# A hybrid SSM and attention block: the order of instructions on every engine read from a table instead of worked out by a planner in the kernel

## The chip, the cores and the metric

The kernel runs on one core of a Trainium2 chip. Its time is the device time of one execution in microseconds. The kernel before took 1474.67 us (median of three runs, 1472.99 to 1477.0).

## The reference

One layer (DEPTH 1, BATCH 1, 2048 tokens, width 1024, f32) of a block with two mixers side by side, cut to its core:

```python
hn = rmsnorm(h, mix_norm_g)
u, g_ssm, q, k, v, g_attn = split(hn @ w_in)          # six times 512 columns
y_ssm = s5_branch(u, ...) * silu(g_ssm)               # 32 groups of 16 channels, 64 complex states each, then GELU and GLU
y_att = stick_breaking_branch(q, k, v, ...) * silu(g_attn)
h = h + concatenate([y_ssm, y_att]) @ w_out
h = h + sigmoid(rmsnorm(h, ple_norm_g) @ w_ple_gate) * (p @ w_ple_proj)
```

Stick-breaking attention, for each of 8 heads of 64 and each block of 128 queries, causal, with q and k normalised per head:

```python
z = einsum(qb, kb) * scale
log_stay = where(strict, log_sigmoid(-z), 0)
later = cumsum(log_stay, reverse) - log_stay
weights = where(strict, exp(log_sigmoid(z) + later), 0)
out = einsum(weights, vb)
```

## The kernel before, in words

Matrices are multiplied in three passes: every operand is split into a rounded high half and what is left of it (`split`, ACT for the high half in L513, DVE for the low half in L65; weights with their norm's scale in L491 on ACT and L76 on DVE, in `load_w`), and `mm3` (L541 to L543) or `mm3x` (L707 to L709) adds high by high, high by low and low by high in one PSUM bank.

The work goes in stages, which overlap at their edges.

- `phase_u` (0 to about 130 us in the trace) makes u for the SSM in eight tiles of 256 tokens, T=0 to 7, in the banks `ps_u`. For T=0, x is loaded already turned (L561), in pieces, beside the first weights (`wst`, `w_w`), and its norm is applied to the result (`norms`: squares L575 on ACT, sums L577 on POOL, `ps_row`, `rs0`, `dg`). For T=1 to 7 each half tile (128 tokens, L593) is squared (L596 on ACT), normalised (L598 on ACT), turned by 16 transposes on PE (L526, `ps_x`) and split into `xt` (L513 on ACT, L65 on DVE), which is also kept in memory (`hn`, L602). Results leave PSUM in L635 (ACT, `uq`). DVE works beside it on the chain of small tables for the SSM (`ssm_chain`, tiles `ex`, `sc`, `pr`).
- The SSM (130 to 315 us) multiplies with packed matrices of the state space, and `gate_unit` makes its gate (`ps_sg`).
- Attention (315 to 1090 us) goes over four passes of two heads each, skewed against each other. `attn_proj` (L745, `ps_q`) projects one block of 128 tokens; ACT and DVE join its two halves (`part`, `qn`); L756 on POOL takes differences of v after a DMA has put the neighbour row in place (`v`); ACT squares, DVE sums, L507 on POOL raises to the power -1/2 (`rs_qk`), DVE multiplies (`qn<-qn,rs_qk`), PE transposes (`ps_tq`) and q, k and the gate are split. `attn_block` makes the scores (L812, `ps_z`), a sigmoid (ACT L816, `px`), a mask (POOL L819), a running product from the right (DVE L821), transposes (L526, `ps_wt`), copies (L835, `ws`), and multiplies with the differences of v (L843, `ps_o`). Between these lie the units of the GLU (`glu_unit`, `ps_g2` and `ps_v2`, its last product L698 on POOL) and `cross_sums`, which makes sums and differences of weight blocks (L874 to L877 on POOL, tiles `old`) for a seven-product scheme.
- `phase_out` (to 1473 us) multiplies with w_out (`mixed_pair`, `ps_h`) and with the gate's weights (`gated_pair`, `ps_t` for transposes, L1000; `ps_g`, `ps_p`) by the seven products of `cross_products`, with `yr` the split operand.

The program text builds these stages one after the other. The order in which each engine takes its instructions is set afterwards by `arrange`, which chains every engine's instructions by a dependency without a semaphore from each to the next: PE, ACT, DVE, POOL and SP (which issues most of the DMAs) each follow their line. In the kernel before, the line comes from a planner. `plan` reads the data dependencies from the instructions' access patterns and gives each a cost (`duration`). `best_order` runs `list_schedule` six times, forwards over the program with ranks from a backward run: at each step the engine that is free first takes the instruction of best rank that is due, with a bonus of `near=4.0` for PE staying in the same tile shape and a cost of `change=0.09` for leaving it. It keeps the order with the earliest end. Hints in the program text (`first`, `later`, `mark`) move ranks and hold back DMAs, and runs marked `abreast` (the halves of a tiled matmul, transposes) stay together.

Of the kernel before, what the change touches and what calls it, by code (L numbers as in the profile page):

```python
# [18 lines left out]
P = 128  # L19
# [1262 lines left out]
def footprint(ap, offset, shape):  # L1282

    row = 1
    for n in shape[1:]:
        row *= n
    p0, m = offset // row, 1
    f = offset % row + sum((n - 1) * s for s, n in ap[1:] if s < 0)
    for s, n in ap[1:]:
        if s and n > 1:  # L1290
            m = sum(m << (abs(s) * k) for k in range(n)) if n * abs(s) > 64 or m != 1 or s not in (1, -1) else (1 << n) - 1
    return p0, p0 + ap[0][1], m << f


def duration(i, name, outs, ins, psum):

    n = max([a[1] for a in outs + ins] or [1])
    eng = str(i.engine).split(".")[-1]
    if name == "InstDMACopy":
        names = [a.bass_ap.tensor.name for a in i.ins if getattr(a, "bass_ap", None) is not None]  # L1300
        return (0.6 if eng == "Pool" else 0.45), (4.0 if any("ssm_w_glu" in k for k in names) else 0.0)
    if name == "InstMatmult":
        cols, kind = outs[0][1], ins[0][2]
        if i.is_transpose:
            return (0.031 if ins[0][0] <= 64 else 0.109), 0.11
        if "float32r" in kind or "bfloat16" in kind:
            return max(cols / 2400.0 + 0.0136, 0.107) / (2 if ins[0][0] <= 64 else 1), 0.11
        half = min(outs[0][0], ins[0][0]) <= 64
        return (0.5 if outs[0][0] <= 32 else 1 if half else 2) * max(cols / 1160.0, 0.056), 0.12
    if eng == "Activation":  # L1310
        return (0.05 if psum else 0.094) + n * 0.00083, 0.065 if psum else 0.03
    if eng == "Pool":
        if name == "InstTensorTensor" and "pow" in str(i.op).lower():
            return 0.35 + 0.15 * n, 0.08
        base, slope = {"InstMemset": (0.04, 0.0008), "InstTensorCopy": (0.4, 0.001), "InstTensorScalarPtr": (0.25, 0.001), "InstTensorScalarAffineSelect": (0.14, 0.0008)}.get(name, (0.12, 0.00186))
        return base + slope * n, 0.09
    if name == "InstTensorScalarPtr" and i.is_tensor_tensor_scan:
        return 0.05 + n * 0.0022, 0.03
# [304 lines left out]
```

## Time and profile before

| | before |
|---|---|
| median of three runs | 1474.67 us |
| profiled execution | 1474.24 us |
| its span in the trace | 1472.5 us |
| mean granted clock of TensorE | 0.994 |
| busy: PE, DVE, ACT, POOL | 98%, 69%, 55%, 32% |
| instructions | 33586 |
| HBM read, written | 166.94 MB, 64.90 MB |

All rows of the trace come from the one profiled execution; its own time is longer than the span since a start and an end lie around the span. A row of the timeline gives start and length in us, the engine, the line, what is written and read, and in brackets the idle time ahead of it with what ended it. PE is busy when any matmul is under way, and matmuls overlap, so the pace is read from start to start.

### The profile page before, as it was taken

Reading aid. Unit: us, or ns where it says so; the run is one execution under the profiler, and the core shown is the slowest. Engines: PE = TensorE matmul, PEld = TensorE weight load, DVE = VectorE, ACT = ScalarE, POOL = GpSimd, SP = SyncE. Lnnn points to the kernel's source line nnn. Section 1 sums busy time; section 2 is a strip of 40 time slices with the busy share of each in tenths; the row PEclk is TensorE's granted clock in tenths of the full one; section 3 lists DMA queues with packets and bytes.
Section 4 is the critical chain, followed back from the end, with each engine's and each line's share of the span. In section 5 each row is a group of like instructions: output and inputs, shape, how many; then the busy total and the mean of one; then the engine's idle time right before and its main releaser. Section 6 shows DMA issues by size and latency. Waiting matters only on the chain.

```text
span 1472.5 us, 33586 instructions
## 1 busy us (share of the span) xinstructions
PE 1436.7 (98%) x13068; PEld 1224.2 (83%) x13068; DVE 1009.0 (69%) x1817; ACT 810.4 (55%) x1765; POOL 474.8 (32%) x512
## 2 busy tenths in 40 slices
PE   6999999999999999999999999999999999999998
PEld 5999889988888888888888877777778888778786
DVE  8953977977567786678766775666778557754444
ACT  5654555565555766567655665555665345533432
POOL 3131363522221211221121124443334554534432
PEclk8999999999999999999999999999999999999999
DMA  8886845645333433334332455766568556523221
GB/s 289 288 287 205 250 143 186 206 143 168 128 130 125 144 112 114 114 130 140 121 126 102 142 146 171 226 218 178 155 201 280 176 171 200 166 65 101 93 72 58
DMA packets 179054, 238.21 MB, mean 162 GB/s; under 512 B 65760, under 2 KB 121296, under 8 KB 167760
## 3 DMA queue, kind: packets, MB, share of 16 engines
q1 hardware_dynamic: 176512, 227.49, 48.0%
q0 software_dynamic: 2384, 8.59, 2.0%
q8 instruction: 103, 1.69, 0.5%
q14 instruction: 55, 0.45, 0.1%
HBM read 166.94 MB, written 64.90 MB: 157 GB/s over the span
## 4 chain that ended last, share of the span: by engine, by line
PE 81%; DVE 7%; DMA 3%; ACT 3%; issue 3%; POOL 2%; SPq 1%; POOLq 0%; DVEq 0%; ACTq 0%
PE ps_q L745 21%; PE ps_o L843 7%; PE ps_z L812 6%; PE ps_wt L526 4%; PE ps_g L707 4%; PE ps_h L709 4%; PE ps_h L707 3%; PE ps_h L708 3%; PE ps_g L709 3%; PE ps_g L708 3%; DMA v<-qn 2%; PE ps_u L541 1%; PE ps_u L543 1%; PE ps_u L542 1%; PE ps_sg L541 1%
## 5 line engine op out<-in xcount | busy, mean ns | idle before, releaser
L821 DVE TENSOR_TENSOR_SCAN px<-px,ps_z 128x512 f32<-128x512 f32 (+3 forms) x320 | 339.9, 1086 | 85.9 <-ACT px L816 61.0
L745 PE MATMUL ps_q<-w_w,xt 64*128 64x512 f32 x2784 | 376.7, 399 | 1.3 <-DVE qn L65 0.7
L745 PEld LDWEIGHTS ps_q<-w_w,xt 64*128 64x128 f32 x2784 | 270.8, 185 | 39.7 <-DVE qn L65 2.2
L816 ACT ACTIVATE px<-ps_z 128x512 f32<-128x512 f32 (+3 forms) x320 | 159.2, 535 | 81.0 <-PE ps_z L812 79.8
L835 ACT ACTIVATE ws<-ps_wt 128x512 f32<-128x512 f32 (+3 forms) x320 | 160.7, 539 | 72.0 <-PE ps_wt L526 67.1
L812 PE MATMUL ps_z<-k,q 64*128 64x512 f32 (+3 forms) x960 | 137.7, 379 | 3.7 <-DVE px L821 1.8
L843 PE MATMUL ps_o<-ws,v 128*64 128x128 f32 x2176 | 134.9, 276 | 0.0
L843 PEld LDWEIGHTS ps_o<-ws,v 128*64 128x64 f32 x2176 | 117.3, 137 | 17.6 <-issue 14.7
L507 POOL TENSOR_TENSOR rs_qk<-rs_qk,mhalf 128x4 f32<-128x4 f32 x64 | 67.7, 1058 | 150.7 <-DVE rs_qk L72 148.1
L526 PEld LDWEIGHTS ps_wt<-ident,px 64*128 64x128 f32 x2176 | 95.5, 138 | 24.3 <-ACT ws L835 5.2
L812 PEld LDWEIGHTS ps_z<-k,q 64*128 64x128 f32 x960 | 87.9, 186 | 21.7 <-issue 5.4
L526 PE MATMUL ps_wt<-ident,px 64*128 64x64 f32 x2176 | 100.7, 224 | 2.0 <-ACT ws L835 1.8
L819 POOL TENSOR_SCALAR_AFFINE_SELECT px<-px 128x128 f32<-128x128 f32 x128 | 40.7, 328 | 164.2 <-ACT px L816 154.3
L756 POOL TENSOR_TENSOR v<-qn,v 128x128 f32<-128x128 f32 x64 | 32.2, 503 | 167.6 <-DMA v<-qn 153.9
L541 PE MATMUL ps_u<-xt,w_w 128*128 128x256 f32 x256 | 76.0, 298 | 7.5 <-ACT w_w L491 6.2
L65 DVE TENSOR_TENSOR yr<-sx,yr 128x512 fp32r<-128x512 f32 x64 | 50.6, 814 | 42.2 <-ACT yr L513 41.8
L543 PE MATMUL ps_u<-xt,w_w 128*128 128x256 f32 x256 | 74.5, 297 | 1.9 <-DVE w_w L76 1.8
L542 PE MATMUL ps_u<-xt,w_w 128*128 128x256 f32 x256 | 75.3, 295 | 0.5 <-DVE xt L65 0.5
L1032 POOL TENSOR_TENSOR sg<-sg,h 128x512 f32<-128x512 f32 x28 | 40.1, 1437 | 92.1 <-DVE sg L65 91.9
L513 ACT ACTIVATE yr<-sx 128x512 fp32r<-128x512 f32 x64 | 39.1, 627 | 53.7 <-POOL sx L912 22.6
L65 DVE TENSOR_TENSOR qn<-ps_q,part 128x512 f32<-128x512 f32 x54 | 36.8, 682 | 42.6 <-ACT part L751 39.0
L513 ACT ACTIVATE yr<-yq 128x512 fp32r<-128x512 f32 x48 | 30.2, 629 | 53.3 <-PE ps_h L709 24.5
(438 smaller groups left out, 3486.5 us busy)
## 6 DMA issues: line engine op xcount, KB each, us to landing
xt<-hn SPq DMA_DIRECT2D x58, 1024.0 KB
hn<-xt SPq DMA_DIRECT2D x16, 1024.0 KB
h<-h SPq DMA_DIRECT2D x64, 256.0 KB
wst<-in_w_in_dram SPq DMA_DIRECT2D x48, 256.0 KB
xg<-hn SPq DMA_DIRECT2D x12, 1024.0 KB
out_dram<-sg SPq DMA_DIRECT2D x31, 256.0 KB
x<-in_x_dram SPq DMA_DIRECT2D x14, 512.0 KB
h<-in_x_dram SPq DMA_DIRECT2D x28, 256.0 KB
```

Of the source, the lines that this page charges most:

```text
L526: e.nc.tensor.transpose(ps[h][:, 64 * k:64 * k + 64], v[r], e.ident[r, r])
L541: mm(out, wh, xh, start=first, stop=False)
L542: mm(out, wh, xl, start=False, stop=False)
L543: mm(out, wl, xh, start=False, stop=last)
L707: mm(out, xh, wh, start=first, stop=False, skip_group_check=more)
L709: mm(out, xl, wh, start=False, stop=last, skip_group_check=more)
L745: nc.tensor.matmul(o, xt[r, a, c], A.w[c][r, b], start=c + s == 0, stop=c == NC8 - 1 and s == 2)
L812: nc.tensor.matmul(z[:, :n], q[half[h], a], A.k[ch][half[h], b, :n], start=s == 0, stop=s == 2)
L816: nc.scalar.activation(px[:, :n], z[:, :n], AF.Sigmoid, scale=-(HD ** -0.5))
L821: nc.vector.tensor_tensor_scan(rv, rv, z[:, :n][:, ::-1], initial=1.0 if carry[h] is None else carry[h], op0=ALU.mult, op1=ALU.bypass)
L835: nc.scalar.activation(dst, ps, AF.Copy, bias=1.0, scale=-1.0)
L843: nc.tensor.matmul(po[half[h], :P], A.v[sb][:, h], w[:, h, b], start=sb == i, stop=sb == 0)
```

## The change

The planner is gone: `footprint`, `duration`, `i_tt`, `plan`, `slots_space`, `shares`, `seen_footprint`, `list_schedule`, `flip` and `best_order` are deleted. In their place stands a table, `_ORDER`, of compressed numbers: for each engine in turn, each number says which of the instructions still left in the program's order comes next. `written_order` reads it and `arrange` chains the lines as before. The first 1278 lines, all that builds instructions, are the same, and so are the instructions. The hints in the program text stay but nothing reads them.

```diff
-def plan(tc, pools):
...
-def list_schedule(ops, pre, soft, length, mode, rank, near=4.0, change=0.09):
...
-def best_order(ops, pre, soft, length, mode, rows, turns=6):
...
+_ENGINES = ("PE", "DVE", "Activation", "Pool", "SP")
+_ORDER = (
+    'c-pmGX{;pIRX+FD+ST3F)ywO*zt?Z=H*c9Y`;0yI^We$Y<8j8Gc*c%N#*;<H3XX-GMOK*Dj<YIGAR;V50u%+vf)cPIfrx|<3Pj2e5P}~l0tq36'
...
+)
+
+
+def written_order(ops):
+
+    import base64, zlib
+    code = iter(zlib.decompress(base64.b85decode(_ORDER)))
+    for e in _ENGINES:
+        left = [i for i in ops if type(i).__name__ != "BassTilePoolBoundary" and str(i.engine).split(".")[-1] == e]
+        line = []
+        while left:
+            at, shift, c = 0, 0, 128
+            while c & 128:
+                c = next(code)
+                at |= (c & 127) << shift
+                shift += 7
+            line.append(left.pop(at))
+        yield line
+
+
 def arrange(tc, pools, rows):
-    ops, pre, *rest = plan(tc, pools)
-    _, order, _ = best_order(ops, pre, *rest, rows)
     info = mybir.DependencyInfo(mybir.DependencyClass.NoSync, mybir.DependencyReason.DATA)
-    for line in order.values():
+    for line in written_order(list(tc.nc.cur_bb.bb.instructions)):
         for a, b in zip(line, line[1:]):
-            tc.add_manual_dep(ops[b], ops[a].name, info, reason="arrange")
+            tc.add_manual_dep(b, a.name, info, reason="arrange")
```

What the table moves is seen in the engines' lines. Over the whole program most of PE's instructions stand within a few microseconds of work of their old place. Three places follow; a name's number tells one tile of a name from another.

**DVE in the start**, from row 104 on before. `w_w` are the low halves of the first weights, `sc` and `pr` belong to the chain for the SSM, `rs0` and `rs_x` to the norms of T=0 and T=1:

```order
L76 SCALAR_TENSOR_TENSOR sc_c_447<-sc_z_445,sc_c_447 128x32
L72 TENSOR_SCALAR sc_h_448<-sc_w_450 128x32
L70 TENSOR_SCALAR sc_c_447<-sc_c_447 128x32
L70 TENSOR_SCALAR sc_h_448<-sc_h_448 128x32
L65 TENSOR_TENSOR pr_den_549<-pr_t1_550,pr_t2_551 128x32
L76 SCALAR_TENSOR_TENSOR w_w_245<-wst_246,gmix_150,w_w_245 128x512
L76 SCALAR_TENSOR_TENSOR w_w_250<-wst_251,gmix_150,w_w_250 128x512
L72 TENSOR_SCALAR rs0_148<-ps_row_261 128x1
L72 TENSOR_SCALAR rs_x_289<-ss_287 128x1
```

DVE from row 66 on in the changed kernel:

```order
L76 SCALAR_TENSOR_TENSOR w_w_213<-wst_214,gmix_150,w_w_213 128x512
L76 SCALAR_TENSOR_TENSOR w_w_218<-wst_219,gmix_150,w_w_218 128x512
L76 SCALAR_TENSOR_TENSOR sc_h_448<-sc_j_443,sc_h_448 128x32
L76 SCALAR_TENSOR_TENSOR w_w_229<-wst_230,gmix_150,w_w_229 128x512
L72 TENSOR_SCALAR rs0_148<-ps_row_261 128x1
L76 SCALAR_TENSOR_TENSOR w_w_245<-wst_246,gmix_150,w_w_245 128x512
L76 SCALAR_TENSOR_TENSOR w_w_234<-wst_235,gmix_150,w_w_234 128x512
L76 SCALAR_TENSOR_TENSOR w_w_250<-wst_251,gmix_150,w_w_250 128x512
```

The last of the eight weights, `w_w_250`, stood at row 110 behind the long chain of small steps, and stands at row 73 now; the norm of T=0 (`rs0`) has moved with it.

**ACT at the change from T=2 to T=3 in phase u**, from row 48 on before. `xt_1054` is T=3's tile, `ps_x0_1096` and `ps_x1_1097` the transposes of its second half, `uq` the evacuations of T=2's results (`ps_u_1119` to `ps_u_1122`):

```order
L513 ACTIVATE xt_1054<-ps_x0_1064 128x8x64
L513 ACTIVATE xt_1054<-ps_x1_1065 128x8x64
L598 ACTIVATE x_1224<-x_1224,rs_x_1229 128x1024
L635 ACTIVATE uq_777<-ps_u_1119 128x16x16
L596 ACTIVATE jk_1258,ss_1259<-x_1256 128x1024
L513 ACTIVATE xt_1054<-ps_x0_1096 128x8x64
L513 ACTIVATE xt_1054<-ps_x1_1097 128x8x64
L635 ACTIVATE uq_778<-ps_u_1120 128x16x16
L598 ACTIVATE x_1256<-x_1256,rs_x_1261 128x1024
L635 ACTIVATE uq_779<-ps_u_1121 128x16x16
```

ACT from row 49 on in the changed kernel:

```order
L491 ACTIVATE w_w_2033<-wst_2034,gmix_150 128x512
L491 ACTIVATE w_w_2038<-wst_2039,gmix_150 128x512
L635 ACTIVATE uq_779<-ps_u_1121 128x16x16
L635 ACTIVATE uq_780<-ps_u_1122 128x16x16
L635 ACTIVATE uq_778<-ps_u_1120 128x16x16
L635 ACTIVATE uq_777<-ps_u_1119 128x16x16
L513 ACTIVATE xt_1054<-ps_x0_1096 128x8x64
L513 ACTIVATE xt_1054<-ps_x1_1097 128x8x64
```

The two splits of the second half stood ahead of three of the four evacuations; now they stand behind all four. On PE the transposes of that half (`x_1087`) stood 49 matmuls ahead of the end of T=2; now all of T=2's matmuls come first, then the transposes, then the first matmul that reads `xt_1054`. At the start, the listing of SP shows the first four pieces of x ahead of the first weight and of `gmix`, where before `gmix` came first and two pieces of x took turns with two weights.

**POOL late in the attention**, from row 365 on before. `old_16914` and `old_16915` are the tiles of one block of `cross_sums`, `rs_qk_16155` the power in the norm of the last projection but one, `v_15800` a difference of v, and L698 the last product of a unit of the GLU:

```order
L874 TENSOR_TENSOR old_16914<-old_16914 128x512
L875 TENSOR_TENSOR old_16914<-old_16915,old_16914 128x512
L876 TENSOR_TENSOR old_16915<-old_16915,old_16914 128x512
L756 TENSOR_TENSOR v_15800<-qn_16090,v_15800 128x128
L507 TENSOR_TENSOR rs_qk_16155<-rs_qk_16155,mhalf_146 128x4
L877 TENSOR_TENSOR old_16915<-old_16915 128x512
L698 TENSOR_TENSOR old_16190<-old_16190 128x512
L819 AFFINE_SELECT px_16281<-px_16281 128x128
L819 AFFINE_SELECT px_16287<-px_16287 128x128
```

POOL from row 364 on in the changed kernel:

```order
L874 TENSOR_TENSOR old_16914<-old_16914 128x512
L875 TENSOR_TENSOR old_16914<-old_16915,old_16914 128x512
L876 TENSOR_TENSOR old_16915<-old_16915,old_16914 128x512
L877 TENSOR_TENSOR old_16915<-old_16915 128x512
L507 TENSOR_TENSOR rs_qk_16155<-rs_qk_16155,mhalf_146 128x4
L756 TENSOR_TENSOR v_15800<-qn_16090,v_15800 128x128
L698 TENSOR_TENSOR old_16190<-old_16190 128x512
L874 TENSOR_TENSOR old_17174<-old_17174 128x512
L875 TENSOR_TENSOR old_17174<-old_17175,old_17174 128x512
L876 TENSOR_TENSOR old_17175<-old_17175,old_17174 128x512
```

The power (L507) stood behind the difference of v and ahead of the last of the four sums; now it stands behind the whole block of sums and ahead of that difference. The masks that came next stand behind the next block of sums.

More of the change, by code (lines that the diff above doesn't have):

```diff
@@ L1279, in hybrid_block_kernel @@
     wstack.close()
[L1282 to L1318, printed above, removed]
-    if name in ("InstMemset", "InstTensorCopy", "InstTensorScalarPtr") and not psum and not i_tt(i):
-        return 0.07 + n * 0.0006, 0.03
-    return 0.07 + n * 0.00104, 0.03
@@ L1432, in slots_space @@
-def slots_space(slots, tag):
-    return slots[tag][0][0]
-def shares(i, name, read, psum):
-    eng = str(i.engine).split(".")[-1]
-    if eng == "Pool":
-        return read > 0 and name != "InstDMACopy"
-    return eng == "DVE" and (read > 1 or (read == 1 and not psum and name in ("InstTensorCopy", "InstTensorScalarPtr")))
-_seen = {}
-def seen_footprint(ap, offset, shape):
-    key = ap, offset, shape
-    if key not in _seen:
-        _seen[key] = footprint(ap, offset, shape)
-    return _seen[key]
```

264 lines of the change are left out of this document (69 added, 195 removed).

## The prediction

> **What bounds the kernel now.** I read the page first, for the share of each engine, then the busy time by stage, then the waits of PE, and last the rows around the longest of them. The page:
>
> ```profile
> span 1472.5 us, 33586 instructions
> PE 1436.7 (98%) x13068; PEld 1224.2 (83%) x13068; DVE 1009.0 (69%) x1817; ACT 810.4 (55%) x1765; POOL 474.8 (32%) x512
> ```
>
> TensorE is busy for all but 1472.5 - 1436.7 = 35.8 us. An order that leaves every instruction as it is can take away idle time, can change how closely matmuls follow each other, and can add idle time; it can't take work away. The stages, where the first number after the length is PE's busy time and PEclk is the granted clock:
>
> ```profile
> core 0: us, PE busy (x) PEld busy (x) DVE busy (x) ACT busy (x) POOL busy (x), PEclk, DMA share, GB/s
> 0.00:40.00 40.00, 26.44 (x163) 24.01 (x164) 35.19 (x188) 23.30 (x40) 15.21 (x28) 0.83 0.82 290
> 40.00:140.00 100.00, 99.17 (x938) 95.94 (x937) 62.37 (x180) 52.98 (x99) 21.59 (x20) 1.00 0.81 272
> 140.00:310.00 170.00, 167.44 (x1339) 157.49 (x1338) 142.04 (x249) 95.68 (x219) 73.78 (x42) 1.00 0.59 183
> 310.00:650.00 340.00, 335.48 (x4083) 286.99 (x4083) 235.50 (x423) 203.94 (x504) 68.46 (x132) 1.00 0.40 133
> 650.00:930.00 280.00, 278.24 (x3367) 233.28 (x3365) 201.24 (x327) 171.65 (x402) 65.90 (x104) 1.00 0.45 135
> 930.00:1090.00 160.00, 155.55 (x1433) 123.38 (x1429) 102.73 (x137) 93.94 (x189) 65.24 (x66) 0.99 0.62 190
> 1090.00:1290.00 200.00, 198.17 (x954) 161.45 (x953) 143.22 (x200) 103.63 (x208) 98.86 (x72) 1.00 0.62 203
> 1290.00:1473.00 183.00, 176.22 (x809) 141.63 (x807) 86.70 (x119) 65.25 (x108) 65.74 (x48) 1.00 0.24 78
> ```
>
> The idle time, length less busy, is 13.6 us in the first 40, then 0.8 and 2.6; 4.5, 1.8 and 4.5, together 10.8, in the attention stages from 310 to 1090; and 1.8 and 6.8 in the output stages. The first stage alone shows a lower clock (0.83). What PE waited for, in sum, count and longest:
>
> ```profile
> PE ps_u L541 <- ACT w_w L491: 6.2, 1, 6.2
> PE ps_g L707 <- ACT yr L513: 2.8, 6, 1.2
> PE ps_tq L526 <- DVE qn L65: 2.2, 2, 1.3
> PE ps_wt L526 <- ACT ws L835: 1.8, 4, 0.6
> PE ps_u L543 <- DVE w_w L76: 1.8, 2, 1.5
> PE ps_q L745 <- DVE gsq L65: 1.6, 1, 1.6
> PE ps_u L541 <- ACT xt L513: 1.2, 1, 1.2
> ```
>
> The 6.2 us are the start, before any weight is there; no order of PE takes them away. The others are ten or so single places, each a chain over ACT, DVE or POOL that came up short of matmuls to hide it. So the question is which of these places the table covers, and which new ones it opens.
>
> **The change, part by part.** *The start.* Three places in PE's rows carry it: the wait for the weights' low half, the start of the second 256 tokens (T=1), and, for the pace, neighbouring rows of one line.
>
> ```profile
> 18.21 0.61 PE L543 MATMUL ps_u<-xt,w_w 128*128 128x256 f32 x3 [1.54 <-DVE w_w L76]
> 33.72 0.58 PE L541 MATMUL ps_u<-xt,w_w 128*128 128x256 f32 x1 [1.17 <-ACT xt L513]
> 34.81 0.58 PE L542 MATMUL ps_u<-xt,w_w 128*128 128x256 f32 x1 [0.51 <-DVE xt L65]
> 35.19 0.42 PE L543 MATMUL ps_u<-xt,w_w 128*128 128x256 f32 x1
> 35.41 0.42 PE L541 MATMUL ps_u<-xt,w_w 128*128 128x256 f32 x1
> 40.10 0.28 PE L541 MATMUL ps_u<-xt,w_w 128*128 128x256 f32 x1
> 40.22 0.28 PE L542 MATMUL ps_u<-xt,w_w 128*128 128x256 f32 x1
> ```
>
> And the same stretches as windows, with the granted clock behind the five engines:
>
> ```profile
> 19.20:22.40 3.20, 3.20 (x16) 3.20 (x16) 3.20 (x13) 2.92 (x4) 1.70 (x2) 0.50 0.70 287
> 33.70:39.50 5.80, 5.27 (x23) 4.98 (x24) 5.78 (x30) 4.02 (x6) 1.81 (x2) 0.50 0.93 379
> ```
>
> At full clock one matmul follows the other by 40.22 - 40.10 = 0.12 us, at the clock of 0.50 by about 0.21 (35.41 - 35.19 = 0.22). A gap of 1.54 us at 18.2 is followed, a microsecond later, by 16 matmuls at half pace: 16 x 0.09 = 1.4 us. The row at 35.19 belongs to 23 such: 2.1 us. In the table, DVE's low halves of the weights come one after the other (the last at row 73, before at 110, behind the chain for the SSM), so the wait of 1.54 and its half pace should go: -2.9. Against it SP loads the first four pieces of x ahead of the first weight and of gmix; one such load more or less ahead of the first weight I put at +0.5, between nothing and the 1.54 us above. ACT has three more steps for T=2 ahead of T=1's last split, so T=1's own wait (1.17 + 0.51) stays in the sum, and of its 2.1 us of half pace I take half: -1.0. Start: -3.4, with -6 (both waits and both half paces gone: 1.5 + 1.4 + 1.7 + 2.1 = 6.7, less 0.5) and +1.5 as ends.
>
> *Phase u, T=2 to 7.* Before, the transposes of a tile's second half stand 49 matmuls (5.9 us by the pace of 0.12) ahead of the matmuls that need them. In the table the transposes of T=3's second half are the last thing ahead of its first matmul, and the four evacuations of T=2 stand ahead of the split on ACT. What lies in that chain:
>
> ```profile
> 32.58 1.08 ACT L513 ACTIVATE xt<-ps_x 128x512 fp32r<-128x512 f32 x2 [1.20 <-PE ps_x L526]
> L635 ACT ACTIVATE uq<-ps_u 128x256 f32<-128x256 f32 x28 | 10.5, 380 | 19.3 <-PE ps_u L543 19.1
> L65 DVE TENSOR_TENSOR xt<-ps_x,xt 128x512 fp32r<-128x512 f32 x28 | 18.0, 684 | 13.8 <-ACT xt L513 13.8
> ```
>
> The last evacuation takes 0.38 and the two splits 1.08, beside 0.7 us of transposes that run at once; the first matmul then waits for ACT and the second for DVE, as at 33.72 and 34.81. I take those two waits as the price, 1.17 + 0.51 = 1.7, and the same half pace as after 18.2, 1.4: +3.1. The bounds: 0.7 (the evacuation's 0.38 and one split of 0.54, less the overlap) and 1.7 + 2.1 = 3.8. [...] The other boundaries keep 1.7 to 3.6 us of matmuls between transposes and use (T=2 1.7, T=4 to 7 2.1 to 3.6, counted in the order at 0.12 each), against a chain of about 1.08 + 0.68 and the hand-overs: 0.5 for T=2 and 0.2 for each of the four others, +1.3. The banks of ps_u come round with 1.9 us between evacuation and reuse (median, 9.1 before), above the 0.38 of one evacuation: nothing. The first batch of the SSM has 3 us less of matmuls ahead of it (16.8 for 19.6) for the way of u through memory; no wait is there before; 0 to 3, I take +0.3, since 0.8 is all the idle time of 40 to 140.
>
> *Attention.* The longest waits, and POOL and DVE at the last two:
>
> ```profile
> 315.51 0.73 PE L745 MATMUL ps_q<-w_w,xg 64*128 64x512 f32 x4 [1.57 <-DVE gsq L65]
> 958.90 0.34 PE L526 MATMUL ps_tq<-ident,qn 64*128 64x64 f32 x4 [1.29 <-DVE qn L65]
> 1019.53 0.34 PE L526 MATMUL ps_tq<-ident,qn 64*128 64x64 f32 x4 [0.87 <-DVE qn L65]
> 1021.54 1.85 PE L812 MATMUL ps_z<-k,q 64*128 64x512 f32 x6 [1.60 <-DVE px L821]
> ```
>
> ```profile
> 1016.43 0.46 POOL L756 TENSOR_TENSOR v<-qn,v 128x128 f32<-128x128 f32 x1 [2.79 <-DMA v<-qn]
> 1016.85 1.01 POOL L507 TENSOR_TENSOR rs_qk<-rs_qk,mhalf 128x4 f32<-128x4 f32 x1
> 1017.83 1.28 POOL L877 TENSOR_TENSOR old<-old 128x512 f32<-128x512 f32 x1
> 1019.06 1.45 POOL L698 TENSOR_TENSOR old<-old 128x512 f32<-128x512 f32 x1
> ```
>
> ```profile
> 1017.89 1.50 DVE L65 TENSOR_TENSOR qn<-qn,rs_qk 128x256 f32<-128x256 f32 x1 [3.98 <-POOL rs_qk L507]
> ```
>
> At 1016 the power on POOL (L507) stands behind a difference that waits 2.79 us for a DMA, then DVE's product waits 3.98 for it, and PE 0.87 and 1.60 for that chain. In the table the power stands ahead of that difference, and the block that follows starts later in PE's order: both waits go. Over all of the attention, PE's work between a projection and the transposes that need it grows (smallest 3.5 to 7.7 us, median 8.6 to 16.2), and between a score and its transposes (one in twenty below 4.1, now 8.3): the 1.29 at 958 goes too, and of the 1.57 at 315 all but 0.3, since 2.8 us of matmuls stand there for 1.3. So -0.87 - 1.60 - 1.29 - 1.27 = -5.0, and of the other 10.8 - 5.3 = 5.5 us of scattered idle time I take a third, -1.8. Shorter now is the way from the transposes of the weights to ps_o:
>
> ```profile
> L835 ACT ACTIVATE ws<-ps_wt 128x512 f32<-128x512 f32 (+3 forms) x320 | 160.7, 539 | 72.0 <-PE ps_wt L526 67.1 <-PE ps_o L843 4.5
> ```
>
> Two copies, 2 x 0.54 = 1.1 us and the hand-overs, lie in it. 29 places have under 3.5 us of matmuls there (10 before), none clearly under 1.3: +1.0, between 0 and 29 x 0.2 = 5.8. PE changes the shape of its tiles 246 times for 238, and comes to ps_o less often from ps_q; +0.5, between -2 and +2.
>
> *140 to 310 and the end.* Of the 2.6 us idle in the SSM I take 1.0, as covers there grow in part only. The six waits for yr, 2.8, are chains from ps_t over ACT; the smallest cover grows from 1.8 to 4.3 us: -2.0. The drain behind the last matmul is the same.
>
> The sum: -3.4 - 5.0 - 1.8 - 1.0 - 2.0 = -13.2, and +3.1 + 1.3 + 0.3 + 1.0 + 0.5 = +6.2; together -7.0. The profiled execution took 1474.24 us, 0.4 below the median of 1474.67, and 1.7 above its span; 1474.24 - 7.0 gives **1467**.
>
> **The rivals.** *All waits go and none comes* (0.17). For it: most covers grow at once, and 35.8 - 6.2 (start) - 4.0 (the last stage's 6.8 less yr's 2.8, the drain above all) = 25.6 us are there to be had. Against it: some covers shrink. 21 of the 25.6 us gone: 1453.
>
> *The waits only move* (0.18). In place of the difference at 1016, POOL has the whole next block of four sums ahead of a mask and the difference ahead of L698 in five places, before three: a wait of 2.79 for a DMA or of a few us for a load then lies in another chain. If that gives back the 6.8 of the attention: 1474.
>
> *Phase u breaks at each tile* (0.20, the slower side). If the chain from the transposes over ACT and DVE is longer than the 1.7 to 3.6 us left to it, all six boundaries from T=2 to T=7 stall like T=1 did: 6 x (1.7 + 1.4) = 18.6 instead of the 4.4 in the sum, +14.2: 1481. It decides from the fourth boundary on: three more at 3.1 take the gain of 7.0. For it: ACT is at 4.02 of 5.8 us at T=1 and holds scale, squares and evacuations in line with the splits. Against it: the window from 40 to 140 has ACT busy for 53 of 100.
>
> That the order isn't what runs I give nothing: the table sets every engine's line, and the listing shows the moved rows.
>
> **How the numbers follow.** Forecast 0.45, all waits gone 0.17, moved 0.18, broken 0.20. Its own range is 1460 to 1472, its ends from start (-6) and T=3, and from the start at +1.5. The range for 8 in 10 reaches to the rivals on both sides, 1450 to 1481. What a measurement of this kernel can tell from no change is 0.3%, 4.4 us: faster is below 1470.3, slower above 1479.1. Faster: 0.40 of the forecast and 0.17; same: 0.05, 0.13 and 0.02 of the last; slower: 0.05 of the third and 0.18: 0.57, 0.20, 0.23.
>
> **What would show it.** In the changed kernel's profile: no wait for w_w L76 above 0.5 and T=1's first ps_u at about 32 us; one wait of some 1.7 for xt at T=3 with PEclk 0.5 behind it, and none like it at T=4 to 7; no wait for qn L65 or px L821 above 0.5; idle time from 310 to 1090 of about 4 us; yr's waits under 1. It would be wrong if PE's busy time, not its idle time, moved by over 3 us, if several boundaries of phase u show xt, or if a wait for rs_qk or px behind POOL's sums stands in the attention.

## The result, and the profile after

| | before | changed |
|---|---|---|
| median | 1474.95 us (4 runs, 1472.99 to 1477.0) | 1517.55 us (4 runs, 1514.11 to 1519.7) |
| profiled execution, span | 1474.24, 1472.5 us | 1518.83, 1516.8 us |
| mean granted clock | 0.994 | 0.984 |

The ratio is 1.0286 (95% interval 1.0261 to 1.0312): 43 us slower. The forecast was 7 us faster, 1467, and the time lies above its range.

First the page of the changed kernel, its span and busy times:

```profile
span 1516.8 us, 33540 instructions
PE 1445.1 (95%) x13068; PEld 1226.5 (81%) x13068; DVE 1030.9 (68%) x1817; ACT 811.8 (54%) x1765; POOL 468.6 (31%) x512
```

PE's idle time is 1516.8 - 1445.1 = 71.7 us, twice the 35.8 of before, and its busy time is 8.4 higher for the same matmuls. Then its windows, cut as before (PE's busy time, and PEclk three numbers from the end):

```profile
0.00:40.00 40.00, 20.12 (x137) 18.05 (x137) 33.62 (x152) 22.37 (x38) 15.20 (x27) 0.93 0.70 246
40.00:140.00 100.00, 85.97 (x774) 81.62 (x775) 70.50 (x206) 47.37 (x86) 15.57 (x17) 0.93 0.68 238
140.00:310.00 170.00, 163.87 (x1288) 153.60 (x1288) 125.32 (x214) 85.92 (x197) 67.54 (x41) 0.99 0.63 187
650.00:930.00 280.00, 267.64 (x3256) 223.95 (x3254) 196.28 (x326) 166.54 (x401) 50.58 (x97) 0.98 0.40 120
```

Phase u, where the idle time was 0.8 us of 100, has 14.0 now, and DVE is busy 70.50 there for 62.37, with 206 steps for 180: it has done 152 in the first 40 us, before 188, so steps come later. In the attention from 650 to 930 the idle time is 12.4 for 1.8. PE's longest waits, in sum, count and longest:

```profile
PE ps_x L526 <- DVE xt L65: 9.7, 5, 7.0
PE ps_u L541 <- ACT w_w L491: 9.0, 2, 7.9
PE ps_wt L526 <- ACT ws L835: 7.4, 8, 3.4
PE ps_x L526 <- DVE pwi L65: 5.9, 1, 5.9
PE ps_sg L541 <- DVE sg L65: 4.5, 2, 4.0
PE ps_tq L526 <- ACT g L791: 3.8, 3, 3.3
```

Windows shift as a kernel falls behind. So for the next table PE's instructions in both traces are counted at one fixed price for each shape, and the times are compared at which the same amount of work is done. Its rows are estimates, good to a microsecond or so:

| place in the changed kernel | lag gained, us |
|---|---|
| first matmul | +1.7 |
| rest of start and phase u, to 125 us | +20.4 |
| 282 us, SSM's gate | +5.8 |
| 704 to 731, weights of the GLU | +8.0 |
| 882 to 887 | +6.4 |
| 994, POOL's block of sums | +4.7 |
| 1030 to 1060 | -5.2 |
| 1138, first products with w_out | +4.2 |
| the rest of the output stage | about -4 |
| everywhere else together | +2 |
| end | +44.0 |

Half the loss is in the first 125 us. These are PE's rows at the change from T=2 to T=3 there:

```profile
79.00 0.36 PE L526 MATMUL ps_x<-ident,x 64*128 64x64 f32 x1 [6.98 <-DVE xt L65]
79.60 1.11 PE L526 MATMUL ps_x<-ident,x 64*128 64x64 f32 x15 [0.23 <-DVE xt L65]
81.79 0.79 PE L541 MATMUL ps_u<-xt,w_w 128*128 128x256 f32 x2 [1.08 <-ACT xt L513]
```

The last wait is the one forecast (1.17). The one of 6.98 wasn't forecast: transposes of the second half wait for the banks `ps_x`, which DVE's low halves of the first half still read. ACT's high halves of that first half, and DVE's line behind them (first and last rows of the chain for the SSM, `tabs` and `cm`):

```profile
68.03 1.09 ACT L513 ACTIVATE xt<-ps_x 128x512 fp32r<-128x512 f32 x2 [5.64 <-PE ps_x L526]
```

```profile
69.09 1.14 DVE L65 TENSOR_TENSOR tabs<-cm,cm 128x256 f32<-128x256 f32 x2
70.06 0.55 DVE L65 TENSOR_TENSOR cm<-tabs 128x32 f32<-128x32 f32 x3
...
77.67 0.68 DVE L65 TENSOR_TENSOR bbs<-bbs,tb 128x512 f32<-128x512 f32 x1
78.27 0.68 DVE L65 TENSOR_TENSOR xt<-ps_x,xt 128x512 fp32r<-128x512 f32 x1
```

ACT is done by 69.12, and DVE waits for nothing, yet it takes the split up at 78.27: 9 us of steps that nobody on PE needs yet stand ahead of it. T=1 shows the same, smaller: its split runs at 34.91 behind such steps, and PE waits 5.90. Behind the gap of 6.98 the granted clock is 0.55, and from 86 us on it is 1.00:

```profile
81.70:86.00 4.30, 4.17 (x19) 3.88 (x20) 4.23 (x5) 0.04 (x1) 0.00 (x0) 0.55 1.01 318
86.00:95.00 9.00, 8.93 (x95) 8.46 (x94) 8.85 (x16) 5.91 (x10) 2.56 (x3) 1.00 0.73 255
```

19 matmuls at half pace (starts 0.21 apart at 84.3, 0.12 at 86.1) are 19 x 0.09 = 1.7 us more. The later places of the table show the same: the granted clock is 0.50 for 3.4 us from 283.6, 3.3 from 713.7, 6.6 from 884.4, 6.7 from 993.6 and 3.3 from 1140.4. So a place costs more than its wait (at 282 us a wait of 3.95 and a loss of 5.8), and PE's busy time grows with it, by 8.4 in all.

### The profile page after: what moved, and what is told of

It reads as the page before. It is cut to its first block, busy times and chain, and to the rows that moved or that the text cites. A ratio compares the mean times of both kernels' runs of the same rounds, so it can differ in the third digit from the quotient of the medians.

```text
span 1516.8 us, 33540 instructions
## 1 busy us (share of the span) xinstructions
PE 1445.1 (95%) x13068; PEld 1226.5 (81%) x13068; DVE 1030.9 (68%) x1817; ACT 811.8 (54%) x1765; POOL 468.6 (31%) x512
## 4 chain that ended last, share of the span: by engine, by line
PE 71%; DVE 11%; DMA 6%; issue 4%; ACT 4%; POOL 2%; SPq 1%; POOLq 0%; DVEq 0%; ACTq 0%
PE ps_q L745 20%; PE ps_o L843 6%; PE ps_z L812 6%; PE ps_wt L526 4%; PE ps_g L707 3%; PE ps_g L708 3%; PE ps_g L709 3%; PE ps_h L709 2%; PE ps_h L707 2%; PE ps_h L708 2%; DMA wst<-in_w_in_dram 1%; PE ps_u L541 1%; PE ps_u L543 1%; PE ps_u L542 1%; DVE cm L65 1%
## 5 line engine op out<-in xcount | busy, mean ns | idle before, releaser
L745 PE MATMUL ps_q<-w_w,xt 64*128 64x512 f32 x2784 | 369.7, 400 | 3.2 <-DVE old L76 3.1
L835 ACT ACTIVATE ws<-ps_wt 128x512 f32<-128x512 f32 (+3 forms) x320 | 155.3, 537 | 68.0 <-PE ps_wt L526 66.9
L507 POOL TENSOR_TENSOR rs_qk<-rs_qk,mhalf 128x4 f32<-128x4 f32 x64 | 65.5, 1023 | 264.2 <-DVE rs_qk L72 264.2
L843 PE MATMUL ps_o<-ws,v 128*64 128x128 f32 x2176 | 140.2, 280 | 2.4 <-DVE yat L65 2.4
L526 PEld LDWEIGHTS ps_wt<-ident,px 64*128 64x128 f32 x2176 | 91.0, 139 | 34.6 <-ACT ws L835 16.0
L541 PE MATMUL ps_u<-xt,w_w 128*128 128x256 f32 x256 | 69.6, 302 | 13.5 <-ACT w_w L491 9.0
L542 PE MATMUL ps_u<-xt,w_w 128*128 128x256 f32 x256 | 68.9, 299 | 3.1 <-DVE xt L65 3.1
L543 PE MATMUL ps_u<-xt,w_w 128*128 128x256 f32 x256 | 67.9, 295 | 1.6 <-DVE w_w L76 1.6
L65 DVE TENSOR_TENSOR yr<-sx,yr 128x512 fp32r<-128x512 f32 x64 | 57.2, 911 | 10.4 <-ACT yr L513 10.0
L541 PEld LDWEIGHTS ps_u<-xt,w_w 128*128 128x128 f32 x256 | 49.6, 205 | 15.2 <-ACT w_w L491 9.3
L541 PE MATMUL ps_sg<-xg,w_w 128*128 128x256 f32 x192 | 53.7, 298 | 4.5 <-DVE sg L65 4.5
```

Source lines behind the costliest of these rows:

```text
L526: e.nc.tensor.transpose(ps[h][:, 64 * k:64 * k + 64], v[r], e.ident[r, r])
L541: mm(out, wh, xh, start=first, stop=False)
L542: mm(out, wh, xl, start=False, stop=False)
L543: mm(out, wl, xh, start=False, stop=last)
L745: nc.tensor.matmul(o, xt[r, a, c], A.w[c][r, b], start=c + s == 0, stop=c == NC8 - 1 and s == 2)
L835: nc.scalar.activation(dst, ps, AF.Copy, bias=1.0, scale=-1.0)
```

## Experiments

The table lets each engine's line be set by itself, so every kernel here has the same instructions and only another order. Ratios are against the kernel before, with their 95% interval. U stands for the rows of start and phase u.

### Which stage, and do the losses add up?

```diff
-line = table[engine]
+line = [i for i in before[engine] if i in U] + [i for i in table[engine] if i not in U]     # u_before
+line = [i for i in table[engine] if i in U] + [i for i in before[engine] if i not in U]     # u_after
```

> All engines follow the order of before for the start and phase u (about the first 110 us) and the table's order after that. Theory (each stage loses by itself, 22 us of the 43 in the start and phase u): 1517.6 - 22 = about 1495, between 1491 and 1499. Rival (the later losses only follow from a late phase u): 1475 to 1480. Rival (the loss lies behind phase u): 1512 or more.

> The mirror: the table's order for the start and phase u, the order of before after that. Theory: 1475 + 22 = about 1497, between 1493 and 1501. Rival (later losses follow from a late phase u): 1512 to 1518. Rival (the loss lies behind phase u): below 1480.

Measured: 1498.26 us, ratio 1.0152 (1.0128 to 1.0176), with before's order in U, and 1498.74, 1.0155 (1.0133 to 1.0176), with the table's order there alone. That is 22 and 23 us above before's 1475.99, measured with them, and their sum, 45, is what the whole table loses (43) as far as the intervals tell. Each part loses by itself; that a late start of the attention would bring the others with it is out.

### Which engine's line, in start and phase u?

SP's line of before, so that the loads come in their old order:

```diff
-L561 DMA x<-in_xt_dram 128x256 x4
-L486 DMA wst<-in_w_in_dram 128x512
 L1102 DMA gmix<-in_small_dram 128x8
-L561 DMA x<-in_xt_dram 128x256 x3
+L561 DMA x<-in_xt_dram 128x256 x2
+L486 DMA wst<-in_w_in_dram 128x512 x2
```

> The table's order on every engine, only SP's line of DMAs in the start and phase u is that of before (gmix first, two pieces of x in turn with two weights). Theory (DVE's line makes the loss of phase u): only the later start comes back, 1517.6 less 2 to 4, 1513 to 1516. Rival (loads in another order make phase u late): most of 22 us comes back, 1495 to 1502.

Measured: 1521.29, ratio 1.0311 (1.0296 to 1.0327). Nothing comes back; the order of the loads is not the cause.

DVE's line alone, 23 rows that feed PE moved up in it, the first of them:

```diff
+L72 TENSOR_SCALAR rs_x<-ss 128x1
 L76 SCALAR_TENSOR_TENSOR w_w<-wst,gmix,w_w 128x512
...
 L65 TENSOR_TENSOR sc_w<-sc_j,sc_m 128x32
-L72 TENSOR_SCALAR rs_x<-ss 128x1
```

> The table's order, only DVE's line is changed: 23 steps that feed PE in phase u (the low halves of xt for T=1 to 4 and the norms rs_x) are moved 7 to 119 rows up, ahead of steps of the chain for the SSM; PE's line stays as it is. Theory (DVE's line holds the feeding steps back): the waits of 5.9 and 7.0 us for xt and some of their neighbours go, 13 to 18 us back, 1500 to 1505. Rival (PE's own line, with the transposes right ahead of their use, makes the loss): 4 us back at most, 1513 or more.

Measured: 1536.09, ratio 1.0408 (1.0392 to 1.0423), 18 us slower than the table and not faster. The long wait for ps_x at T=3 did go, but two others came:

```profile
86.48 0.58 PE L542 MATMUL ps_u<-xt,w_w 128*128 128x256 f32 x1 [9.44 <-DVE xt L65]
116.41 0.58 PE L541 MATMUL ps_u<-xt,w_w 128*128 128x256 f32 x1 [10.40 <-ACT uq L635]
```

A split that stands too early holds DVE (5.03 us at 51.92) until its transposes are there, and what stands behind it is late in turn. So the places of 23 rows in DVE's line move the time by 18 us; that DVE's line made the loss, this kernel doesn't show.

So DVE's line was filled anew, each step that feeds PE as soon as it is due and the chain between them, and in POOL's line the powers for `rs_x` went ahead of a product for the SSM and of some transfers; PE's, ACT's and SP's lines stayed the table's:

```diff
+L507 TENSOR_TENSOR rs_x_1402<-rs_x_1402,mhalf_146 128x1
 L638 DMA u0_76<-uq_777 128x16x64
 L638 DMA u1_77<-uq_778 128x16x64
-L507 TENSOR_TENSOR rs_x_1402<-rs_x_1402,mhalf_146 128x1
+L507 TENSOR_TENSOR rs_x_1434<-rs_x_1434,mhalf_146 128x1
```

> The table's order, with two lines changed in phase u only: on DVE each step that feeds PE (xt, rs_x, uq, w_w) is taken as soon as it is due and the chain for the SSM fills the rest (the first try waited 5 us for a split put too early and left others late), and on POOL the powers for rs_x stand ahead of a product for the SSM; PE, ACT and SP keep the table's lines. Theory (the lines of DVE and POOL hold back what feeds PE): at least half of the 22 us back, 1500 to 1508. Rival (PE's own line, transposes right ahead of their use): 1513 or more.

Measured: 1499.33, ratio 1.0157 (1.0127 to 1.0187): 18 of the 22 us are back. With DVE free, its splits start 0.63 us behind ACT's, and T=3 on PE reads, in this kernel:

```profile
69.05 0.50 PE L541 MATMUL ps_u<-xt,w_w 128*128 128x256 f32 x2 [1.17 <-ACT xt L513]
69.88 0.38 PE L542 MATMUL ps_u<-xt,w_w 128*128 128x256 f32 x1 [0.33 <-DVE xt L65]
...
70.86 0.42 PE L541 MATMUL ps_u<-xt,w_w 128*128 128x256 f32 x1
71.07 0.42 PE L542 MATMUL ps_u<-xt,w_w 128*128 128x256 f32 x1
```

The waits are 1.17 + 0.33 = 1.5, and from 70.86 to 74.06 15 matmuls follow at half pace (71.07 - 70.86 = 0.21), 15 x 0.09 = 1.4. So 2.9 is what the transposes' new place next to their use costs by itself (forecast 1.7 + 1.4 = 3.1), and the theory that PE's line had done it all falls. How the 18 us divide between DVE's line and POOL's isn't measured.

A wait of this size doesn't always cost the pace: in the changed kernel one of 1.37 at 59.54 and one of 1.59 at 100.04 are followed by matmuls 0.12 apart, and what decides, no run shows.

### 282 us: DVE beside POOL

In the changed kernel PE waits 3.95 for `sg`, and DVE's products ahead of it are slow while POOL makes its own:

```profile
274.86 2.53 DVE L65 TENSOR_TENSOR rot<-rot,tabs 128x512 f32<-128x512 f32 x1
277.49 2.68 DVE L65 TENSOR_TENSOR rot<-rot,swp 128x512 f32<-128x512 f32 x1
```

```profile
274.49 2.35 POOL L332 TENSOR_TENSOR stC<-pwr,cts 128x1024 f32<-128x1024 f32 x1 [0.63 <-PE ps_y L464]
276.92 2.70 POOL L334 TENSOR_TENSOR stC<-stC,tm 128x1024 f32<-128x1024 f32 x1
```

In the experiment POOL's three products go behind its next one:

```diff
+L413 TENSOR_TENSOR swp_3589<-swp_3589,tabs_3586 128x512
 L332 TENSOR_TENSOR stC_3550<-pwr_500,cts_363 128x1024
 L334 TENSOR_TENSOR stC_3550<-stC_3550,tm2_3551 128x1024
 L333 TENSOR_TENSOR tm2_3802<-pwi_501,cts_363 128x1024
-L413 TENSOR_TENSOR swp_3589<-swp_3589,tabs_3586 128x512
```

> The table's order, only POOL's line is changed at one place: three products of the SSM's pack (L332, L334, L333), which run at 274 to 282 us beside DVE's products for the state, come behind the next swap product instead. Theory (POOL and DVE slow each other there, DVE's products of 0.7 us took 2.5 and 2.7, and the gate's product behind them freed PE's bank late): DVE's products near 0.7, PE's wait of 3.95 for sg gone, 3 to 5 us back, 1512.5 to 1514.5. Rival (the products are slow for another reason): no change, 1516 to 1519.

The same two steps, and then the next of their kind, in this experiment:

```profile
274.17 0.68 DVE L65 TENSOR_TENSOR rot<-rot,tabs 128x512 f32<-128x512 f32 x1
274.95 0.69 DVE L65 TENSOR_TENSOR rot<-rot,swp 128x512 f32<-128x512 f32 x1
...
283.54 2.51 DVE L65 TENSOR_TENSOR rot<-rot,swp 128x512 f32<-128x512 f32 x1 [1.82 <-POOL swp L413]
```

```profile
290.43 0.47 PE L352 MATMUL ps_pack<-ident,lt 128*128 128x128 f32 x1 [3.95 <-ACT lt L349]
```

Mechanism shown: without POOL beside it the step takes 0.68 for 2.53, and PE's wait for sg is gone (-5.8 us there). But the products now run beside another `rot`, PE waits 3.95 at 290 (+7.4), and the whole takes 1515.99, ratio 1.0271 (1.0246 to 1.0295): nothing gained. In the two traces these steps of `rot` take 2.53, 2.68 and 2.51 beside POOL's products L332 and L334, and 0.68 and 0.69 without them; what makes them slow there, no run shows.

### 700 and 885 us: loads, splits, and who waits behind them

At 704 to 712 PE waits 1.97 and 3.36 for copies (`ws`) that stand on ACT behind splits of the GLU's weights, and these wait for their loads:

```profile
704.86 0.71 PE L526 MATMUL ps_wt<-ident,px 64*128 64x64 f32 x16 [1.97 <-ACT ws L835]
...
712.32 0.46 PE L526 MATMUL ps_wt<-ident,px 64*128 64x64 f32 x8 [3.36 <-ACT ws L835]
```

```profile
702.71 0.63 ACT L513 ACTIVATE w_w<-wst 128x512 fp32r<-128x512 f32 x1 [3.09 <-DMA wst<-in_ssm_w_glu_dram]
...
710.67 0.63 ACT L513 ACTIVATE w_w<-wst 128x512 fp32r<-128x512 f32 x1 [3.97 <-DMA wst<-in_ssm_w_glu_dram]
```

```profile
698.24 0.66 SPq L753 DMA_DIRECT2D v<-qn  x1
699.07 5.36 SPq L486 DMA_DIRECT2D wst<-in_ssm_w_glu_dram  x1
704.52 0.69 SPq L847 DMA_DIRECT2D ya<-yat  x1
705.31 7.28 SPq L486 DMA_DIRECT2D wst<-in_ssm_w_glu_dram  x2
```

SP needs 5.36 us for one and 7.28 for two loads of a kind that took 0.64 at 695.03. Three kernels try to get past this place. The first moves ACT's splits (and two of DVE's) to later rows, here and at 885:

```diff
-L513 ACTIVATE w_w_12811<-wst_12812 128x512
+L513 ACTIVATE w_w_12806<-wst_12807 128x512
...
+L513 ACTIVATE w_w_12811<-wst_12812 128x512
 L513 ACTIVATE w_w_12816<-wst_12817 128x512
```

> The table's order, with a few rows moved: on ACT four splits of the GLU's weights, which waited 3.1, 4.0, 1.6 and 1.4 us for their loads, come some rows later, behind copies that PE waits for, and two of DVE's low halves with them. Theory (a step that waits for a load at the head of ACT's line holds back the copies behind it): PE's waits of 2.0, 3.4 and 3.3 us go, 6 to 9 us back, 1508.5 to 1511.5. Rival (the copies are late by themselves, or the loads hold up something else): under 2 us, 1515.5 or more.

Measured: 1518.24, ratio 1.0279 (1.0253 to 1.0306). The 3.34 at 886 goes, but at 712 PE waits 3.45 for DVE's `px`, whose mask stands on POOL behind a difference that waits 5.20 for its DMA. The second keeps the rows at 700 alone and moves that mask as well:

```diff
+L819 AFFINE_SELECT px_10669<-px_10669 128x128
 L756 TENSOR_TENSOR v_10321<-qn_10738,v_10321 128x128
-L819 AFFINE_SELECT px_10669<-px_10669 128x128
```

> The table's order, with the place at 704 to 712 us alone changed: on ACT the two splits that waited 3.1 and 4.0 us for loads and on DVE their low halves come some rows later (as in the run with four splits moved), and on POOL a mask of px comes ahead of the difference of v that stands before it and waits for its DMA (5.2 us in that run). Theory (two lines hold PE back there, ACT's by a load and POOL's by a DMA; with ACT's alone mended POOL's took over): the 8 us of that place go, 1508 to 1511. Rival (the place is bound by the transfers themselves): under 2 us, 1515.5 or more.

Measured: 1516.64, ratio 1.0263 (1.0243 to 1.0283). Again a wait of 3.04 for px at 715.12: now DVE's low half of a late weight stands ahead of the scan. The third moves SP's loads ahead of the copy of v's rows:

```diff
+L486 DMA wst_12812<-in_ssm_w_glu_dram 128x1x512
+L486 DMA wst_12817<-in_ssm_w_glu_dram 128x1x512
 L753 DMA v_10321<-qn_10738 127x128
-L486 DMA wst_12812<-in_ssm_w_glu_dram 128x1x512
 L847 DMA ya4_102<-yat_10315 128x128
-L486 DMA wst_12817<-in_ssm_w_glu_dram 128x1x512
```

> The changed kernel with five rows of SP's line moved: at the place around 700 us the second and third load of the GLU's weights (wst, L486) stand ahead of the copy of v's rows (L753, tile v_10321) instead of behind it, and the two loads of the next set ahead of the pair L755/L753 that follows; all other lines as in the table. Theory that the 8 us lost there start with SP's line (the load's issue takes 5.36 and 7.28 us behind that copy, ACT then waits 3.09 and 3.97 for the load): ACT's waits for wst go, PE's ps_wt waits of 1.97 and 3.36 go, and the time falls by 5 to 8 us against the changed kernel, to about 1511. Rival, that the loads are slow wherever they stand (too much traffic at that time, so that they come as late and another row is held): within 2 us of the changed kernel, 1517, with ACT still waiting 2 to 4 us for wst.

Measured: 1519.63, ratio 1.0299 (1.0277 to 1.032). The theory fell: the issue is slow ahead of the copy too, and though ACT's second wait for a load shrinks to 0.94, DVE's px is late again:

```profile
698.67 5.92 SPq L486 DMA_DIRECT2D wst<-in_ssm_w_glu_dram  x2
```

```profile
704.83 0.71 PE L526 MATMUL ps_wt<-ident,px 64*128 64x64 f32 x16 [2.20 <-ACT ws L835]
714.88 0.48 PE L526 MATMUL ps_wt<-ident,px 64*128 64x64 f32 x4 [4.30 <-DVE px L821]
```

What makes SP slow at 700 us, and a cure for this place, stay open; that the late splits cost the 8 us there is read from the trace and not shown by a run.

### 994 us: a power behind four sums

In the changed kernel POOL's four sums (L874 to L877) wait for loads, and the power whose input DVE wrote at 983.36 stands behind them. DVE waits for the power, and PE for DVE's next step:

```profile
986.55 1.29 POOL L874 TENSOR_TENSOR old<-old 128x512 f32<-128x512 f32 x1 [4.55 <-DMA old<-in_w_out_dram]
...
991.98 1.01 POOL L507 TENSOR_TENSOR rs_qk<-rs_qk,mhalf 128x4 f32<-128x4 f32 x1
```

```profile
993.02 0.42 DVE L65 TENSOR_TENSOR qn<-qn,rs_qk 128x256 f32<-128x256 f32 x1 [5.68 <-POOL rs_qk L507]
```

```profile
994.16 2.07 PE L745 MATMUL ps_q<-w_w,xt 64*128 64x512 f32 x8 [3.09 <-DVE old L76]
```

```diff
+L507 TENSOR_TENSOR rs_qk_15335<-rs_qk_15335,mhalf_146 128x4
 L874 TENSOR_TENSOR old_15914<-old_15914 128x512
...
 L877 TENSOR_TENSOR old_15915<-old_15915 128x512
-L507 TENSOR_TENSOR rs_qk_15335<-rs_qk_15335,mhalf_146 128x4
```

> The table's order, with one row of POOL moved: the power rs_qk that ran at 992 us, 8.6 us after it was due, comes ahead of the block of four sums before it. Theory (the sums ahead of the power make the wait of 3.1 us for old at 994): 3 to 5 us back, 1512.5 to 1514.5. Rival (the power isn't what PE waits for): no change, 1516 to 1519.

Measured: 1516.67, ratio 1.0271 (1.0248 to 1.0294). By the lag PE gains 2.9 at 994 and 2.0 behind it and loses some 3 ahead of the moved row; the time can't be told from the table's. Then all cures together:

```diff
-table's lines
+lines of DVE and POOL in U as above, filled anew
+splits at 700 and 885, mask ahead of L756, power ahead of L874
```

> All repairs at once on the table's order: DVE's and POOL's lines in phase u (18 us back by itself), four splits later on ACT, the mask ahead of the difference and the one power ahead of its sums on POOL; PE's and SP's lines are the table's. Theory (the places add): 1499 less 8 to 14, 1485 to 1491. Rival (a wait that is mended behind phase u comes back at a later place): 1496 to 1501.

Measured: 1502.41, ratio 1.0169 (1.0145 to 1.0193), no better than the cure of U alone. By the lag it wins 1.4 at 282 and 2.3 at 994, nothing at 700, and loses 3.0 at 885. Rows moved by hand, each for the wait that a trace shows, bring nothing that can be measured in this order once phase u is cured.

### The same rule on the kernel before

One row: the power that waits at 1016 behind a difference. Then a second: the power behind four sums at 957 goes behind the first of them.

```diff
+L507 TENSOR_TENSOR rs_qk_16155<-rs_qk_16155,mhalf_146 128x4      # b_pool and b_two
 L756 TENSOR_TENSOR v_15800<-qn_16090,v_15800 128x128
-L507 TENSOR_TENSOR rs_qk_16155<-rs_qk_16155,mhalf_146 128x4
...
+L507 TENSOR_TENSOR rs_qk_15335<-rs_qk_15335,mhalf_146 128x4      # b_two alone
 L875 TENSOR_TENSOR old_15914<-old_15915,old_15914 128x512
```

> The order of before, with one row of POOL moved: the power rs_qk at 1017 us comes ahead of the difference of v that waits 2.8 us for its DMA, as the table has it. Theory of the prediction (the two waits of 0.87 and 1.60 us of PE go): 2.5 us faster than before, 1471.5 to 1473.5. Rival (something else is late next, the sum L877 or the mask): no change, 1474 to 1477.

> The kernel before with two rows of POOL's line moved: the power for qn ahead of the difference of v that waits for a DMA at 1016 us (the one change of the earlier run, which gave -1.9), and the power that stands behind four sums at 957 us moved up behind the first of them (its input is there at 952.72, the second sum begins at 953.25). Theory that a row's place on its own engine's line is what costs: DVE's wait of 5.53 for rs_qk at 958 falls to about 1.5, PE's wait of 1.29 there goes, with the earlier change -3.2 in all, 1471.8. Rival, that a wait taken away there comes back later, since the sums come 1 us later: as the earlier run, -1.9 or less.

Measured: one row 1475.32 for 1477.26, ratio 0.9987 (0.9975 to 0.9999); two rows 1473.43 for 1475.53, ratio 0.9984 (0.9972 to 0.9995). Both gain about 2 us, and the second row's own share can't be told from none by the medians. With one row PE's wait of 0.87 is gone, and of the 1.60 behind it 1.03 is left:

```profile
1023.26 1.54 PE L812 MATMUL ps_z<-k,q 64*128 64x512 f32 x6 [1.03 <-DVE px L821]
```

In the trace of the kernel with two rows DVE's wait at 958 is 1.19 for 5.53 and PE's 1.29 there is gone (with one row, which leaves this place as it was, they are 3.71 and 0.57):

```profile
954.29 1.49 DVE L65 TENSOR_TENSOR qn<-qn,rs_qk 128x256 f32<-128x256 f32 x1 [1.19 <-POOL rs_qk L507]
```

Last, the table's output stage behind that order:

```diff
+line = [i for i in b_two[engine] if i in V] + [i for i in table[engine] if i not in V]     # V: up to about 1125 us
```

> The kernel before's lines with the two POOL rows moved as in the run before (-2.1), up to about 1125 us; from there on, the output stage, every engine's line is the table's. Theory that the gain forecast for the output stage (the waits for yr gone, -2.0) is real, also behind the old order: another -2 to -4 us, the profile without waits for ACT's yr above 0.5, and the time 1469 to 1472, 3 to 6 us below the kernel before. Rival, that the gain seen in the changed kernel there was only time that it had lost at 1138 and got back: within 1 us of the run before, 1473 to 1475.

Measured: 1471.86 for 1476.61, ratio 0.9966 (0.9954 to 0.9978), the fastest of all. PE's waits for ACT's yr come to 0.6 us for 2.8 and the time falls by 4.75 in all, 2.1 of it from the two rows. The rest, some 2.6, is the output stage (1.7 by the lag of the two traces); since the two ratios' intervals overlap, and the two profiled executions have the same span (1468.8 and 1468.7), its size is an estimate.

### A new plan by the old planner

The planner of before once more, with ACT's and DVE's costs from the traces, first without and then with its rule that a DVE step of two SBUF inputs and a POOL product don't overlap:

```diff
-length[k] = duration(...)             # ACT and DVE: from the formula
+length[k] = shorter of the two traces
-port = t + length[k][0]               # replan only; replan_port keeps it
```

> The planner of before, run again with one thing changed: the costs of DVE's and ACT's instructions are the durations of this kernel's traces instead of its formulas (and DVE and POOL don't exclude each other in it); its order is written out as a table. Theory (what a written order is worth hangs on the durations that it was made with): faster than before by 4 to 9 us, 1466 to 1471. Rival (durations aren't what decides, the lines only need slack): 1473 or more.

> The kernel before's planner again, with the durations of ACT and DVE steps taken from the traces as in the run with the new plan, but this time with the planner's rule kept that a DVE step of two inputs in SBUF and a POOL product don't overlap. Theory that the 25 us which the new plan lost in the SSM (150 to 300 us) came from leaving that rule out: those 25 us go, and the time is within 8 us of the kernel before, 1468 to 1484. Rival, that the durations did it, or that any new plan of this planner lands some 20 us off the chosen one: 1492 to 1505, with the loss again in 150 to 300 us.

Measured: 1501.89, ratio 1.0161 (1.014 to 1.0181), and 1501.67, 1.0175 (1.0155 to 1.0195). Leaving the rule out was not the cause. With it the lag grows by 16 us between 155 and 311 us of before and by 11 more to the end of the attention. A second order of the same search, from costs that are right step by step, lands 25 us off too; why is open.

## Why the prediction was wrong

**The method: covers counted in PE's line alone.** The prediction took the pairs on PE (transposes and their use, a projection and its transposes), counted matmuls between them, and called a wait gone where the count grew. That is the step that failed; only at a few places (ACT at T=1 and T=3, POOL at 1016) did it look at what stands ahead on another engine. Between the two stand steps on ACT, DVE and POOL, each a line that is taken in order, and what stands ahead of the step there counts too. At T=3 the chain of 1.08 + 0.68 was priced rightly, and 9 us of other DVE work stood ahead of it: PE waited 6.98. With DVE's and POOL's lines filled anew and PE's kept, 18 us came back. By the traces the same holds on ACT at 704 and 886 (splits that wait for loads, 3.97) and on POOL at 994 (sums that wait for a load, 4.55); there the rows moved by hand gave no time back.

**Start, -3.4.** Wrong in sign: T=1 begins 5.7 us later. The first matmul is 1.7 later. The low halves of the weights did move up, as the listing showed, but PE's rows in the changed kernel read:

```profile
7.89 0.79 PE L541 MATMUL ps_u<-xt,w_w 128*128 128x256 f32 x2 [7.89 <-ACT w_w L491]
...
12.62 0.58 PE L543 MATMUL ps_u<-xt,w_w 128*128 128x256 f32 x1 [1.62 <-DVE w_w L76]
...
39.41 0.58 PE L541 MATMUL ps_u<-xt,w_w 128*128 128x256 f32 x1 [1.08 <-ACT xt L513]
```

A wait for w_w L76 is still there (1.62 for 1.54), now for the first of the low halves, which DVE takes at 11.81 and before at 7.29. And the chain that the weights were moved past now stands ahead of T=1's norm and splits: T=1's first matmul is at 39.41, before at 33.72, forecast about 32. What gains a place in an in-order line takes it from another; the working named who gains and not who loses.

**Phase u, +3.1 and +1.3.** T=3's own waits and half pace were 1.5 + 1.4 = 2.9 with DVE's and POOL's lines filled anew, so the 3.1 was sized well for what it counted. By the lag the place lost some 11 us, since the wait of 6.98 and more of the half pace came on top. The slower rival, phase u breaking, was right on the place and on the sign, and short on the price: with its 18.6 the stage would have lost 18.6 - 3.4 + 0.3 = 15.5, and it lost 22.1. Nor does each tile break: T=1 to T=3 do, and behind them phase u has one more wait of over 1 us (1.59 at 100.04, for an evacuation).

**Attention, -5.0 - 1.8 + 1.0 + 0.5.** The waits of 0.87 and 1.60 did go in the changed kernel (-5.2 at 1030 to 1060), so the mechanism read there was right; the single POOL row on the kernel before gains 1.9 and takes the first of them away. The 2.5 priced was too little, as the half pace behind the wait was left out (the granted clock before was 0.50 from 1022.6 to 1026.0). The prediction gives no source for the 0.5 for eight more changes of tile shape, and no run shows it by itself; in the trace of before a change takes 0.31 to 0.32 from start to start for 0.23 (953.64 to 953.95, 956.19 to 956.51), by that 8 x 0.09 = 0.7. The third taken off the scattered waits was a guess, and it went the other way: three new places in the attention, 8.0 + 6.4 + 4.7 = 19 us, with half pace behind each. The rival "the waits only move" was right at 994, where POOL's block of sums waits for a load and holds the step behind it (it named a mask; it was the power), and it priced this at 6.8 in all.

**SSM, -1.0.** Wrong in sign: 5.8 lost at 282, where DVE's products run beside POOL's. Covers on PE don't show such a collision.

**Output stage, -2.0.** In the changed kernel 4.2 are lost at 1138 and about 4 won behind it, and PE still waits 1.7 for ACT's yr (forecast under 1). Behind the old order the term holds: 0.6 us of waits, and about 2.6 won, by the estimate above.

**What would have shown it.** The text named the signs against itself: PE's busy time moving by over 3 (it moved by 8.4), several boundaries with xt, a wait for rs_qk. All three are in the profile (T=1 to T=3; DVE's 5.68 for rs_qk at 993). The lower end of its own range, 1460, doesn't follow from the ends that it names: 1467 less 2.6 for the start and 2.4 for T=3 is 1462. The chance of 0.23 for slower was too small for a change that moves rows on five lines at once, since any of hundreds of dependent pairs can lose its cover and only the tight ones were looked at.

## What to carry to other kernels

When an order is written out, follow each feeding step back on its own engine: when its input is there, what stands ahead of it in that line, and for what the row at the head of the line waits. Count for every row that moves up who is pushed down; splits taken too early cost as much as splits taken too late (18 us lost with 23 of DVE's rows moved up, 18 us back with DVE's and POOL's lines filled anew). Move single rows where the trace shows a ready step behind a waiting one, and measure each, since here the next wait stood a few microseconds behind (282 and 290 us).

## What the runs showed that was not expected

- The losses of two parts of the order add within the noise (22 and 23, measured apart, for 43 together), though the engines run across the border.
- A wait cured is often given back within 10 us: -5.8 and then +7.4 at 282, and three cures at 700 us with 8 us still lost.
- SP took 5.4 to 7.3 us to issue one or two 128 x 512 loads at 700 us, ahead of the copy of v as behind it; in the kernel before two copies of v take 6.03 (at 691.89) and 6.47 (at 704.70). What SP waits for there, no run shows.
- DVE's steps of 128x32 start 0.22 us apart where one needs the other's result (`pr_dt` and `pr_x` at 10.07 and 10.29 in the changed kernel), and 0.11 apart where not (`pr_x` and `pr_th` at 9.89 and 10.00 before), so DVE takes longer for the same steps when its line has nothing to lay between them.
